# A transformer layer in split fp32: input rows kept on chip as the residual, and operand copies by ScalarE for the feed forward's block sums

## The chip, the cores and the metric

The kernel runs on one core of one Trainium2 chip. The core has five engines that run their own queues of instructions: TensorE (PE, matrix products; its weight loads are listed as PEld), VectorE (DVE), ScalarE (ACT), GpSimd (POOL) and SyncE (SP), which here only issues DMA. Engines wait for each other through semaphores; matrix products land in PSUM banks, everything else lives in SBUF. The metric is device microseconds of one launch.

## The reference

One layer on 512 tokens of width 1024, all in fp32:

```python
h = rms_norm(x, mix_norm_pre)
x = x + rms_norm(hybrid_mixer(h, ...), mix_norm_post)      # w_in, sparse attention, mLSTM, w_out
h = rms_norm(x, xattn_norm_pre)
x = x + rms_norm(memory_cross_attention(h, rms_norm(mem, mem_norm), ...), xattn_norm_post)
h = rms_norm(x, ffn_norm_pre)
g, u = jnp.split(h @ w_gate_up, 2, axis=-1)                # 1024 -> 2 x 2816
x = x + rms_norm((silu(g) * u) @ w_down, ffn_norm_post)
```

The mixer multiplies h by w_in, runs sparse attention over half of the columns and a chunked mLSTM over the other half, and multiplies by w_out. The cross attention reads 256 memory tokens.

## The kernel before

**Products in split fp32.** An fp32 operand is kept as a high and a low part of type fp32r: `split` has ScalarE copy the source to the high part (L166) and VectorE or GpSimd subtract that from the source for the low part (L167). A product is then three matmuls: low times high, high times low, high times high (L285 to L287 in `mm3`, L1210 to L1212 in `product`). Names that end in h or l are the parts: wah and wal (the small columns of w_in), wmh (its mLSTM value columns), hTh and hTl (the normalised input, transposed), wh and wl (a feed forward weight), A and AS (feed forward operands, both parts in one tile).

**Tiles and order.** The 512 tokens are four tiles of 128. The program is written in the order of the computation, and the Tile framework's scheduler, which simulates a time line, then sets the order in each engine's queue. Buffers come from pools with a fixed count; a tile that takes over a buffer waits until the former owner's last reader is done. A table, `PLAN`, holds strings that choose by position which engine does a step: v is VectorE, p is GpSimd.

**The head.** `load_x` has SyncE load the four row tiles of x into two tiles of a pool named S, which has six buffers (`slot`). `prenorm` normalises a row tile: ScalarE squares it and sums the row (L241), the reciprocal root is formed with GpSimd (L235), then for each half of 512 columns either VectorE scales it by root and gain in one pass (L249), or, where the plan says p, ScalarE scales it (L246) and GpSimd multiplies by the gain (L247). TensorE transposes the eight 128 x 128 squares into two PSUM banks (L253, tile name bk_pn), and `H.store` splits each bank into the transposed operand. In the head that operand is hT, four tiles from the same six S buffers, and mvx, the mLSTM values, is another S tile. The first products that use hT are bk_A (w_in's small columns, weights wah and wal) and bk_mv (weights wmh). The input rows are not kept: for the residual the ScalarE queue loads x a second time, into two tiles x1, by the DMA at L1026. That load has no wait, so the scheduler puts it at the start of the queue.

**The feed forward.** `ev_second2` ends the cross attention for a row tile (`post_second`, with the residual update at L282) and runs `prenorm` with the plan string norm3 into the operand A. A has four blocks, 11, 12, 21, 22: token half times feature half, each with both parts. The gate and up weights come in eleven column blocks. Block 0 multiplies A directly. Blocks 1 to 10 (`gate_up(d)`) use a scheme with seven products in place of eight for a 2 x 2 block product: besides 11, 12 and 22 they read four sums of the blocks, S1 = 21 + 22, S2 = S1 - 11, S3 = 11 - 21, S4 = 12 - S2, and sums of the weights (L1257 and its like, on VectorE). Each weight is split as it is needed, most on VectorE; the weights for block 12 (`w21`) and for S3 (`ulo`) are split by GpSimd. The raw weights sit in two pools of two buffers, `fraw[d % 2]`. SyncE loads block d + 2's into a pool when block d's are done with.

`A.sums(i)` forms the S operands for each row tile of 128 tokens. For that it first rebuilds the unsplit blocks by adding the two parts again: GpSimd does 11 and 12 (tile aq, L1186), VectorE does 21 and 22 (tile ar, L1183 and L1186). Row tiles 0 and 1 are the first token half, 2 and 3 the second, and the sums pair tile i with tile i + 2.

After the gate_up blocks come the products with w_down, and a last norm. They are not touched by the change.

Of the kernel before, what the change touches and what calls it, by code (L numbers as in the profile page):

```python
# [8 lines left out]
F32 = mybir.dt.float32  # L9
F32R = mybir.dt.float32r  # L10
AF = mybir.ActivationFunctionType
OP = mybir.AluOpType
AX = mybir.AxisListType

P = 128
S = 512
D = 1024
NT = S // P
# [28 lines left out]
def hybrid_layer(ctx, tc, a, out):  # L47
    nc = tc.nc
# [3 lines left out]
    xp = ENT(tc.tile_pool(name="xp", bufs=2))  # L52
# [22 lines left out]

# [3 lines left out]

# [38 lines left out]
    def norms_on_pool(name):  # L118

        return [(q // 2, q % 2) for q in range(8) if PLAN[name][q] == "p"]  # L120
# [4 lines left out]
    POOL1, POOL2, POOL3 = (norms_on_pool("norm%d" % n) for n in range(1, 4))  # L125
    x, mem = a["x"][0], a["mem"][0]
# [3 lines left out]
    def bank(tag, name=None):  # L130

        if tag == "b":
            tag = "pv" if turn[0] % 4 == 3 else "sc"
            turn[0] += 1
        return ps.tile([P, 512], F32, tag=tag, name=name or "bk_" + tag, bufs=BUFS[tag])

    def slot(shape, dt=F32, name="slot"):
        return sl.tile(shape, dt, tag="S", name=name)
# [22 lines left out]
    def small(shape, name, bufs=2):  # L161
        return sm.tile(shape, F32, tag=name, name=name, bufs=bufs)
# [75 lines left out]
    def prenorm(xi, i, gain, H, tag="tr", pool=(), take=None):  # L238
        ss = small([P, 1], "ss", 4)
        xn = (take or x4)([P, D], name="xn")  # L240
        nc.scalar.activation(xn, xi, AF.Square, scale=1.0 / 32.0, accum_out=ss)  # L241
        r = rstd_of(ss, 1)
        for g in range(2):
            c = slice(512 * g, 512 * g + 512)
            if (i, g) in pool:
                nc.scalar.activation(xn[:, c], xi[:, c], AF.Copy, scale=r)  # L246
                nc.gpsimd.tensor_tensor(xn[:, c], xn[:, c], gain[g], op=OP.mult)  # L247
            else:
                nc.vector.scalar_tensor_tensor(xn[:, c], xi[:, c], r, gain[g], op0=OP.mult, op1=OP.mult)  # L249
            b = bank(tag, "bk_pn")  # L250
            for k in range(4):
                kk = 4 * g + k
                nc.tensor.transpose(b[:, 128 * k:128 * k + 128], xn[:, 128 * kk:128 * kk + 128], ident)  # L253
            b3 = b.rearrange("p (k t) -> p k t", k=4)
            H.store(g, 128 * i, 128 * i + 128, b3)
# [108 lines left out]
    H = Big()  # L364
# [8 lines left out]
    mvx = slot([P, NT, 4, 129], name="mvx")  # L373
    nc.gpsimd.memset(mvx[:, :, :, 128:129], 1.0)
    wa, wm = [], []
    xin = [None] * NT

    def load_x(i):
        if i % 2 == 0:
            xin[i] = slot([P, 2, D], name="xin")  # L380
            xin[i + 1] = xin[i][:, 1, :]
            xin[i] = xin[i][:, 0, :]
        nc.sync.dma_start(xin[i], x[128 * i:128 * i + 128, :])

    def load_a(g):
        raw = rawt([P, 4, 288])
# [27 lines left out]
    g_in = []  # L414
# [36 lines left out]
        return nB[h][:, last:r0 + 1:step][:, ::-1]  # L451

    for i in range(NT):
        prenorm(xin[i], i, g_in, H, pool=POOL1)
    nc.sync.dma_start(gb, a["mlstm_gate_bias"][0].rearrange("(o i) h -> o (i h)", o=1).to_broadcast([P, 8]))
    nc.sync.dma_start(rows[0:16], a["conv_w"][0].rearrange("w (c p) -> (w c) p", p=P))
    nc.sync.dma_start(rows[16:20], a["conv_b"][0].rearrange("(c p) -> c p", p=P))
# [82 lines left out]
    for j in range(NT):  # L540
        for i in range(j, NT):
            idx[i, j] = len(idx)
            c = 4 * idx[i, j]
            src = ir[:, 128 * j:128 * j + 128]
            if i > j:
# [6 lines left out]
                src = t  # L552
# [416 lines left out]
    def comp_loads(n):  # L969
        for g in range(2):  # L970
            comp_load(n, g)

    whole = {"c0": lambda: conv(0), "c1": lambda: conv(1),
             "m0": lambda: start("m0", 2336, 2, H, ev_mo(0)), "m2": lambda: start("m2", 2336 + 256, 2, H, ev_mo(2)),
             "kc": lambda: start("kc", 512, 2, H, ev_kcvc),
             "ks": lambda: start("ks", (768, 1024), 2, H, lambda j, b: ev_k(j)(0, b)),
             "q0": lambda: start("q0", 0, 2, H, ev_q(0)),
             "Ck": lambda: comp("k"), "Cv": lambda: comp("v")}
    begun = {}
    for op in PLAN["order"].split():  # L980
# [4 lines left out]
        else:  # L985
            n = op[1]
# [34 lines left out]

    g_post = gain_bc(a["mix_norm_post"])
    g_pre = gain_bc(a["xattn_norm_pre"])
    x1 = [xp.tile([P, 2, D], F32, tag="x1", name="x1") for _ in range(2)]
    for i in range(2):
        nc.scalar.dma_start(x1[i], x[256 * i:256 * i + 256, :].rearrange("(i p) c -> p i c", p=P))  # L1026

    def res(i):
        return x1[i // 2][:, i % 2, :]

    w_out = a["w_out"][0]
    first = {}

# [80 lines left out]
    fraw = [pool("fr0", 2, "right")]  # L1114
# [8 lines left out]
    def weights(src, eng=None):  # L1123
        w = wtile(name="wh"), wtile(name="wl")
        split(*w, src, eng)
        return w
# [10 lines left out]
    def gtile(shape=(P, 2, 512), name="gf"):  # L1137
        return fg.tile(list(shape), F32, tag="gf", name=name)
# [4 lines left out]
    class Blocks:  # L1143
# [29 lines left out]
        def store(self, g, c0, c1, src):  # L1173
            i = c0 // 128
            self.put("%d%d" % (i // 2 + 1, g + 1), i, src)

        def whole(self, o, n, i, eng):

            c = slice(128 * (i % 2), 128 * (i % 2) + 128)
            if n == "21":  # L1180
                for k in (0, 2):
                    h, l = (self.piece(n, q, k)[:, :, c].bitcast(F32) for q in range(2))
                    eng.tensor_tensor(o[:, k:k + 2], h, l, op=OP.add)  # L1183
            else:
                h, l = (self.c[n][:, q, :, c].bitcast(F32) for q in range(2))
                eng.tensor_tensor(o, h, l, op=OP.add)  # L1186

        def sums(self, i):
            q, r, s = (gtile((P, 2, 4, 128), name=n) for n in ("aq", "ar", "as"))
            for n in range(2):  # L1190
                self.whole(q[:, n], "1%d" % (n + 1), i, nc.gpsimd)
                self.whole(r[:, n], "2%d" % (n + 1), i, nc.vector)
            nc.vector.tensor_tensor(s[:, 0], r[:, 0], r[:, 1], op=OP.add)
            nc.vector.tensor_tensor(s[:, 1], s[:, 0], q[:, 0], op=OP.subtract)
            self.put("S2", i, s[:, 1])
            self.put("S1", i, s[:, 0])
            nc.vector.tensor_tensor(r[:, 0], q[:, 0], r[:, 0], op=OP.subtract)
            self.put("S3", i, r[:, 0])
            nc.vector.tensor_tensor(q[:, 1], q[:, 1], s[:, 1], op=OP.subtract)
            self.put("S4", i, q[:, 1])  # L1200

    def product(b, w, n, start, stop=True):

# [22 lines left out]
    A = Blocks()  # L1226
# [2 lines left out]

    w_first = [weights(q) for q in load_gu(0)]  # L1230

    def ev_second2(i, b):
        post_second(first[i], b, g_post2, res(i), res(i), pn=sgran)
        prenorm(res(i), i, g_pre2, A, pool=POOL3, take=ntile)
# [11 lines left out]
    def gate_up(d):  # L1246

        glo, ghi, ulo, uhi = load_gu(d)
        X, Y = bank("sc", "bk_X"), bank("d", "bk_Y")
        product(X, weights(glo), "11", True)  # L1250
        x1 = etile(name="x1")
        nc.scalar.activation(x1, X, AF.Copy)
        w21 = weights(ghi, nc.gpsimd)
        t1 = ft.tile([P, 4, 256], F32, tag="t1", name="t1")
        nc.vector.tensor_tensor(t1, ulo, glo, op=OP.subtract)
        nc.vector.tensor_tensor(ulo, uhi, ulo, op=OP.subtract)
        nc.vector.tensor_tensor(glo, ulo, glo, op=OP.add)  # L1257
        product(Y, w21, "12", True)
        nc.vector.tensor_tensor(x1, x1, Y, op=OP.add)
        nc.scalar.activation(x1, x1, AF.Silu)  # L1260
        product(X, weights(glo), "S2", False)
        u2 = etile(name="u2")
        nc.scalar.activation(u2, X, AF.Copy)  # L1263
        Z = bank("pv" if d % 2 else "tr", "bk_Z")
        product(Z, weights(t1), "S1", True)
        p5 = etile(name="p5")
        nc.scalar.activation(p5, Z, AF.Copy)
        nc.vector.tensor_tensor(ghi, ghi, glo, op=OP.subtract)  # L1268
        product(X, weights(ulo, nc.gpsimd), "S3", False)
        nc.vector.tensor_tensor(p5, p5, X, op=OP.add)  # L1270
        product(Z, weights(uhi), "S4", False)
        nc.vector.tensor_tensor(u2, u2, Z, op=OP.add)
        Gf[d] = gtile()
        nc.gpsimd.tensor_tensor(Gf[d][:, :, 0:256], halves(x1), halves(u2), op=OP.mult)
        product(X, weights(ghi), "22", False)
        s2 = etile(name="s2")
        nc.scalar.activation(s2, X, AF.Silu)
        nc.gpsimd.tensor_tensor(Gf[d][:, :, 256:512], halves(s2), halves(p5), op=OP.mult)

    Gf[0] = gtile()  # L1280
    for t in range(2):
# [4 lines left out]
        s1 = etile(name="s1")  # L1286
        nc.scalar.activation(s1, gate, AF.Silu)
        nc.vector.tensor_tensor(Gf[0][:, :, 256 * t:256 * t + 256], halves(s1), halves(up), op=OP.mult)
    for i in range(2, NT):
        A.sums(i)  # L1290
    for d in range(1, NF // 2):
        gate_up(d)

# [6 lines left out]
    for g in range(NF // 2):  # L1300
        raw = fraw[1 - g // 2 % 2].tile([P, 2, D], F32, tag="raw", name="raw")
        nc.sync.dma_start(raw, wd[:, 2 * g:2 * g + 2, :])
        for q in range(2):
            k = 2 * g + q
# [11 lines left out]
            for i in range(NT):  # L1316
                t = slice(128 * i, 128 * i + 128)
                for n in range(2):
                    c = slice(512 * n, 512 * n + 512)
                    mm3(bk[i][n], gs[:, 0, t], gs[:, 1, t], hi[:, c], lo[:, c], k == 0, False)  # L1320
    for i in range(NT):
        t = slice(128 * i, 128 * i + 128)
        for n in range(2):
            c = slice(512 * n, 512 * n + 512)
# [4 lines left out]
        for n in range(2):  # L1329
            c = slice(512 * n, 512 * n + 512)  # L1330
# [30 lines left out]
```

## Time and profile before

| | us |
|---|---|
| three runs | 860.01, 865.17, 865.51 |
| median | 865.17 |
| the profiled execution | 864.1 |
| its span | 862.3 |

The profiled execution had 12,664 instructions and a mean granted clock of TensorE of 0.99. The page cuts the span into 40 slices of 21.6 us; a digit is the busy share of an engine in a slice, in tenths (9 is 90% or more), and PEclk is the clock that TensorE was granted. These lines give the shape of the whole program: the head is the first slice or two, the feed forward starts in the 24th and ends with the last.

```profile
PE   5899999998999999999999988999999999999997
DVE  3528687688879835843453689788888884323413
ACT  5423565667857743733453435444554444324311
POOL 3405133255437542511320255444444445322420
PEclk9999998999999999999999999999999999999999
DMA  8633332331102242252341330333333333322101
```

TensorE is under 0.9 in the first two slices, in one in the mixer (the 10th), around the opening of the feed forward, and at the very end. In the timeline view a row has the start, the time in us, the engine (a name with q is that engine's issue of DMA or its sequencer), the line, the operation, out<-in, the size, and in brackets the idle time ahead of it with what ended it. Rows of like instructions in a row are joined (x2), and their time is then that of all.

### The profile page before, as it was taken

How to read it: one execution, taken by the hardware profiler on the slowest of the kernel's cores; microseconds unless marked ns; L12 is line 12 of the kernel's file. 1: busy time of each engine (PE TensorE's matmuls, PEld its weight loads, DVE VectorE, ACT ScalarE, POOL GpSimd, SP SyncE). 2: the span in 40 equal slices, each digit the busy share in tenths (PEclk: the TensorE clock that was granted, in tenths of full speed). 3: DMA queues.
4: the chain of work that ended last, by engine and by line, in shares of the span. 5: the costliest groups of instructions: out<-in, count | busy, mean ns of one | idle time of the engine just before them, and what ended most of it. 6: DMA issues, size and time to landing. Idle time of an engine off the chain costs nothing. (4 is left out here: it accounts for less than half of the span.)

```text
span 862.3 us, 12664 instructions
## 1 busy us (share of the span) xinstructions
PE 822.5 (95%) x4833; PEld 707.7 (82%) x4833; DVE 543.1 (63%) x925; ACT 424.3 (49%) x838; POOL 326.9 (38%) x238
## 2 busy tenths in 40 slices
PE   5899999998999999999999988999999999999997
PEld 3787677885688978778888887999999999888885
DVE  3528687688879835843453689788888884323413
ACT  5423565667857743733453435444554444324311
POOL 3405133255437542511320255444444445322420
PEclk9999998999999999999999999999999999999999
DMA  8633332331102242252341330333333333322101
GB/s 274 208 110 115 84 91 62 105 103 50 52 24 84 98 139 72 80 165 69 127 147 49 102 119 1 99 98 98 99 107 116 115 122 130 99 98 98 50 25 73
DMA packets 68307, 85.27 MB, mean 99 GB/s; under 512 B 4400, under 2 KB 53905, under 8 KB 68246
## 3 DMA queue, kind: packets, MB, share of 16 engines
q1 hardware_dynamic: 64574, 77.97, 27.9%
q10 hardware_dynamic: 3672, 6.50, 2.2%
q8 instruction: 38, 0.62, 0.3%
q14 instruction: 23, 0.19, 0.1%
HBM read 82.34 MB, written 2.12 MB: 98 GB/s over the span
## 5 line engine op out<-in xcount | busy, mean ns | idle before, releaser
L166 ACT ACTIVATE whi<-raw 128x1024 fp32r<-128x1024 f32 (+1 forms) x80 | 76.8, 967 | 69.6 <-PE bk_dT L285 31.9
L167 DVE TENSOR_TENSOR wlo<-raw,whi 128x1024 fp32r<-128x1024 f32 x41 | 55.0, 1343 | 80.1 <-PE bk_ff L286 43.0
L166 ACT ACTIVATE wh<-raw 128x1024 fp32r<-128x1024 f32 x64 | 67.3, 1057 | 60.6 <-PE bk_X L1210 24.5
L167 POOL TENSOR_TENSOR wl<-raw,wh 128x1024 fp32r<-128x1024 f32 x20 | 62.8, 3143 | 89.9 <-ACT wh L166 89.9
L167 POOL TENSOR_TENSOR wlo<-raw,whi 128x1024 fp32r<-128x1024 f32 x23 | 56.2, 2443 | 93.9 <-ACT whi L166 92.1
L285 PE MATMUL bk_dT<-hTh,wlo 128*128 128x512 f32 x192 | 77.4, 403 | 1.4 <-DVE wlo L167 0.8
L287 PE MATMUL bk_dT<-hTh,whi 128*128 128x512 f32 x192 | 76.8, 400 | 0.0
L286 PE MATMUL bk_dT<-hTl,whi 128*128 128x512 f32 x192 | 76.6, 399 | 0.0
L167 DVE TENSOR_TENSOR wl<-raw,wh 128x1024 fp32r<-128x1024 f32 x44 | 63.3, 1444 | 10.3 <-ACT wh L166 10.3
L167 POOL TENSOR_TENSOR gs<-gf,gs 128x512 fp32r<-128x512 f32 x22 | 32.8, 1498 | 65.4 <-ACT gs L166 65.4
L1210 PE MATMUL bk_X<-A,wl 128*128 128x256 f32 x192 | 54.4, 283 | 0.5 <-ACT A L166 0.5
L1211 PE MATMUL bk_X<-A,wh 128*128 128x256 f32 x192 | 54.4, 283 | 0.3 <-DVE A L167 0.3
L1212 PE MATMUL bk_X<-A,wh 128*128 128x256 f32 x192 | 54.2, 283 | 0.0
L1210 PE MATMUL bk_X<-AS,wl 128*128 128x256 f32 x160 | 46.2, 289 | 4.4 <-ACT u L1263 2.4
L286 PE MATMUL bk_ff<-wlo,gs 128*128 128x512 f32 x128 | 49.8, 389 | 0.0
L287 PE MATMUL bk_ff<-whi,gs 128*128 128x512 f32 x128 | 49.6, 389 | 0.0
L285 PE MATMUL bk_ff<-whi,gs 128*128 128x512 f32 x128 | 47.4, 389 | 0.0
L891 POOL TENSOR_SCALAR s<-s,acf 128x128 f32<-128x128 f32 (+3 forms) x32 | 36.3, 1145 | 25.6 <-PE bk_tr L906 15.9
L1212 PE MATMUL bk_X<-AS,wh 128*128 128x256 f32 x160 | 45.6, 285 | 0.0
L1211 PE MATMUL bk_X<-AS,wh 128*128 128x256 f32 x160 | 45.5, 285 | 0.0
L285 PEld LDWEIGHTS bk_dT<-hTh,wlo 128*128 128x128 f32 x192 | 36.3, 189 | 10.8 <-DVE wlo L167 1.9
L1210 PE MATMUL bk_Z<-AS,wl 128*128 128x256 f32 x160 | 45.0, 281 | 0.0
(375 smaller groups left out, 2566.8 us busy)
## 6 DMA issues: line engine op xcount, KB each, us to landing
raw<-in_w_gate_up_dram SPq DMA_DIRECT2D x22, 1024.0 KB, 5.6
raw<-in_w_down_dram SPq DMA_DIRECT2D x11, 1024.0 KB, 5.3
raw<-in_w_xkv_dram SPq DMA_DIRECT2D x8, 1024.0 KB, 5.0
raw<-in_w_in_dram SPq DMA_DIRECT2D x7, 1024.0 KB, 6.1
raw<-in_w_out_dram SPq DMA_DIRECT2D x4, 1024.0 KB, 5.2
raw<-in_w_xq_dram SPq DMA_DIRECT2D x4, 1024.0 KB
raw<-in_w_xo_dram SPq DMA_DIRECT2D x4, 1024.0 KB, 5.1
raw<-in_w_in_dram SPq DMA_DIRECT2D x6, 512.0 KB, 4.0
```

What stands on the lines that cost most here:

```text
L166: nc.scalar.activation(hi, src, AF.Copy)
L167: (eng or nc.vector).tensor_tensor(lo, src, hi.bitcast(F32), op=OP.subtract)
L285: nc.tensor.matmul(o, lhsT=wl, rhs=xh, start=start, stop=False)
L286: nc.tensor.matmul(o, lhsT=wh, rhs=xl, start=False, stop=False)
L287: nc.tensor.matmul(o, lhsT=wh, rhs=xh, start=False, stop=stop)
L891: ENG[on].tensor_scalar(s[:, 0:n], s[:, 0:n], c, None, op0=OP.mult)
L1210: nc.tensor.matmul(o, lhsT=wl[:, k, c], rhs=A.hi(n, k), start=st, stop=False, skip_group_check=True)
L1211: nc.tensor.matmul(o, lhsT=wh[:, k, c], rhs=A.lo(n, k), start=False, stop=False, skip_group_check=True)
L1212: nc.tensor.matmul(o, lhsT=wh[:, k, c], rhs=A.hi(n, k), start=False, stop=stop and k == 3, skip_group_check=True)
```

## The change

Two parts.

First, the rows of x are loaded into two tiles `xres` of the pool that held x1, and `res(i)` reads them from the start of the program: `prenorm` of the head normalises them, and the later residual update adds to them in place. The second load and the tiles x1 are gone, and the two input tiles of the S pool with them.

Second, in the opening of the feed forward, norm3 becomes "vvvvvvvv": all eight half tiles of that norm are scaled by VectorE in one pass, none by ScalarE and GpSimd. `Blocks.store`, besides the split, has ScalarE copy the PSUM bank as it is into a tile `aw`. The two aw tiles are taken from the raw weight pool of the even blocks, `fraw[0]`. `Blocks.whole()` with its additions is gone, and `sums()`, now called once for all tiles, forms the four sums on VectorE from aw, S3 and S4 in place. For block 1 alone the split of `w21` moves from GpSimd to VectorE.

```diff
-        "norm3": "vpvpppvv",
+        "norm3": "vvvvvvvv",
...
-    xin = [None] * NT
+    xres = [xp.tile([P, 2, D], F32, tag="x", name="xin") for _ in range(2)]
+
+    def res(i):
+
+        return xres[i // 2][:, i % 2, :]

     def load_x(i):
-        if i % 2 == 0:
-            xin[i] = slot([P, 2, D], name="xin")
-            xin[i + 1] = xin[i][:, 1, :]
-            xin[i] = xin[i][:, 0, :]
-        nc.sync.dma_start(xin[i], x[128 * i:128 * i + 128, :])
+        nc.sync.dma_start(res(i), x[128 * i:128 * i + 128, :])
...
-        prenorm(xin[i], i, g_in, H, pool=POOL1)
+        prenorm(res(i), i, g_in, H, pool=POOL1)
...
-    x1 = [xp.tile([P, 2, D], F32, tag="x1", name="x1") for _ in range(2)]
-    for i in range(2):
-        nc.scalar.dma_start(x1[i], x[256 * i:256 * i + 256, :].rearrange("(i p) c -> p i c", p=P))
...
         def store(self, g, c0, c1, src):
             i = c0 // 128
             self.put("%d%d" % (i // 2 + 1, g + 1), i, src)
+            nc.scalar.activation(self.whole[i // 2][:, i % 2, g], src, AF.Copy)

-        def whole(self, o, n, i, eng):
...
-        def sums(self, i):
-            q, r, s = (gtile((P, 2, 4, 128), name=n) for n in ("aq", "ar", "as"))
-            for n in range(2):
-                self.whole(q[:, n], "1%d" % (n + 1), i, nc.gpsimd)
-                self.whole(r[:, n], "2%d" % (n + 1), i, nc.vector)
...
+        def sums(self):
+            q, r = self.whole
+            s = [gtile((P, 2, 4, 128), name="as") for _ in range(2)]
+            for i in range(2):
+                nc.vector.tensor_tensor(s[i][:, 0], r[:, i, 0], r[:, i, 1], op=OP.add)
+                nc.vector.tensor_tensor(s[i][:, 1], s[i][:, 0], q[:, i, 0], op=OP.subtract)
+                self.put("S2", i, s[i][:, 1])
+            for i in range(2):
+                self.put("S1", i, s[i][:, 0])
+            for i in range(2):
+                nc.vector.tensor_tensor(r[:, i, 0], q[:, i, 0], r[:, i, 0], op=OP.subtract)
+                self.put("S3", i, r[:, i, 0])
+            for i in range(2):
+                nc.vector.tensor_tensor(q[:, i, 1], q[:, i, 1], s[i][:, 1], op=OP.subtract)
+                self.put("S4", i, q[:, i, 1])
...
+    A.whole = [fraw[0].tile([P, 2, 2, 4, 128], F32, tag="raw", name="aw") for _ in range(2)]
...
-        w21 = weights(ghi, nc.gpsimd)
+        w21 = weights(ghi, nc.vector if d == 1 else nc.gpsimd)
...
-    for i in range(2, NT):
-        A.sums(i)
+    A.sums()
```

The scheduler lays the queues out anew. Between the head and the feed forward's opening the order stays as it was. In the listings below, lines of the changed kernel are numbered in its own file, up to 15 less than before.

ScalarE's queue at the head; rows with - stand only before, with + only after. gain is a gain row spread over the partitions, xin an input row tile, bk_pn a bank of transposed squares.

```order
-L1026 DMA x_3425<-in_x_dram 128x2x1024
-L1026 DMA x_3426<-in_x_dram 128x2x1024
 L419 ACTIVATE gain<-bk_g 128x512
 L241 ACTIVATE xn,ss<-xin 128x1024
 L419 ACTIVATE gain<-bk_g 128x512
 L246 ACTIVATE xn<-xin,rs_r 128x512
-L166 ACTIVATE hTh<-bk_pn 128x4x128 x2
-L166 ACTIVATE wah<-raw 128x288 x8
+L166 ACTIVATE wah<-raw 128x288 x4
+L166 ACTIVATE hTh<-bk_pn 128x4x128
+L166 ACTIVATE wah<-raw 128x288 x4
+L166 ACTIVATE hTh<-bk_pn 128x4x128
```

The two DMAs are gone, and the splits of wah moved ahead of those of the first two banks of hT, four before each.

ScalarE's queue as the feed forward opens, before, around the splits of row tiles 0 and 1. A_ with a number is a block of A, pn,ss the square of the cross attention's output for its norm, x_ with a number the residual rows.

```order
L166 ACTIVATE A_4812<-bk_pn 128x4x128
L258 ACTIVATE pn,ss_4986<-bk_dR 128x512
L246 ACTIVATE xn<-x_3425,rs_r 128x512
L166 ACTIVATE A_4813<-bk_pn 128x4x128
L241 ACTIVATE xn,ss<-x_3426 128x1024
L258 ACTIVATE pn,ss_5049<-bk_dR 128x512
L166 ACTIVATE A_4812<-bk_pn 128x4x128
L246 ACTIVATE xn<-x_3426,rs_r 128x512 x2
L166 ACTIVATE A_4813<-bk_pn 128x4x128
L241 ACTIVATE xn,ss<-x_3426 128x1024
```

And the same stretch after:

```order
L166 ACTIVATE A_4808<-bk_pn 128x4x128
L166 ACTIVATE A_4809<-bk_pn 128x4x128
L258 ACTIVATE pn,ss_4986<-bk_dR 128x512
L1169 ACTIVATE aw<-bk_pn 128x512 x2
L241 ACTIVATE xn,ss<-xin 128x1024
L258 ACTIVATE pn,ss_5049<-bk_dR 128x512
L166 ACTIVATE A_4808<-bk_pn 128x4x128
L166 ACTIVATE A_4809<-bk_pn 128x4x128
L1169 ACTIVATE aw<-bk_pn 128x512 x2
L241 ACTIVATE xn,ss<-xin 128x1024
```

The scaling passes of L246 are gone; the two copies to aw (L1169) stand behind the high parts of both banks, ahead of the next row tile's row sum.

VectorE's queue at the start of block 1, before. ar, aq and as are the rebuilt blocks and their sums, AS_ with a number an S operand, raw the weights and their sums, gf the output of a feed forward block.

```order
L167 TENSOR_TENSOR AS_5099<-ar,AS_5099 128x4x128
L1257 TENSOR_TENSOR raw<-raw 128x1024
L167 TENSOR_TENSOR AS_5098<-as,AS_5098 128x4x128
L1199 TENSOR_TENSOR aq<-aq,as 128x512
L167 TENSOR_TENSOR AS_5100<-aq,AS_5100 128x4x128
L167 TENSOR_TENSOR AS_5097<-as,AS_5097 128x4x128
L1288 TENSOR_TENSOR gf<-s_5301,bk_Y 128x2x256
L167 TENSOR_TENSOR AS_5099<-ar,AS_5099 128x4x128
L1268 TENSOR_TENSOR raw<-raw 128x1024
L167 TENSOR_TENSOR wl<-raw,wh 128x1024
```

And after:

```order
L167 TENSOR_TENSOR wl<-raw,wh 128x1024
L167 TENSOR_TENSOR AS_5101<-aw,AS_5101 128x4x128
L167 TENSOR_TENSOR AS_5099<-as,AS_5099 128x4x128
L167 TENSOR_TENSOR AS_5101<-aw,AS_5101 128x4x128
L167 TENSOR_TENSOR AS_5102<-aw,AS_5102 128x4x128
L167 TENSOR_TENSOR wl<-raw,wh 128x1024
L1244 TENSOR_TENSOR raw<-raw 128x1024
L167 TENSOR_TENSOR AS_5102<-aw,AS_5102 128x4x128
L1275 TENSOR_TENSOR gf<-s_5303,bk_Y 128x2x256
L1255 TENSOR_TENSOR raw<-raw 128x1024
L167 TENSOR_TENSOR wl<-raw,wh 128x1024
```

The sums' low parts now come from aw, and of the splits of weights (wl) among them one more belongs to VectorE, w21 of block 1.

More of the change, by code (lines that the diff above doesn't have):

```diff
@@ L1023, in hybrid_layer @@
     g_pre = gain_bc(a["xattn_norm_pre"])
-    x1 = [xp.tile([P, 2, D], F32, tag="x1", name="x1") for _ in range(2)]
-    for i in range(2):
-        nc.scalar.dma_start(x1[i], x[256 * i:256 * i + 256, :].rearrange("(i p) c -> p i c", p=P))
-    def res(i):
-        return x1[i // 2][:, i % 2, :]
     w_out = a["w_out"][0]
@@ L1175, in store @@
             self.put("%d%d" % (i // 2 + 1, g + 1), i, src)
-        def whole(self, o, n, i, eng):
[L1179 to L1186, printed above, removed]
-        def sums(self, i):
-            q, r, s = (gtile((P, 2, 4, 128), name=n) for n in ("aq", "ar", "as"))
-            for n in range(2):
-                self.whole(q[:, n], "1%d" % (n + 1), i, nc.gpsimd)
-                self.whole(r[:, n], "2%d" % (n + 1), i, nc.vector)
[L1193 to L1200, printed above, removed]
+            nc.scalar.activation(self.whole[i // 2][:, i % 2, g], src, AF.Copy)
[14 more added lines that the diff above has]
+                self.put("S4", i, q[:, i, 1])
     def product(b, w, n, start, stop=True):
```

## The prediction

> **What bounds the kernel now.** I read the profile's page first: busy shares, then the chain that ended last. TensorE works nearly all the time and carries the chain; every other engine has room.
>
> ```profile
> PE 822.5 (95%) x4833; PEld 707.7 (82%) x4833; DVE 543.1 (63%) x925; ACT 424.3 (49%) x838; POOL 326.9 (38%) x238
> PE 37%; DVE 3%; issue 1%; ACT 1%; DVEq 0%; POOLq 0%; POOL 0%; ACTq 0%
> ```
>
> So an edit is worth what it takes from TensorE's idle time (862.3 - 822.5 = 39.8 us) or from stretches where its clock is cut. The view by windows, cut where TensorE's timeline changes, shows these (columns: stretch, length, then busy us and count for PE, PEld, DVE, ACT, POOL, then granted clock, DMA share, GB/s).
>
> ```profile
> 0.00:13.00 13.00, 5.95 (x12) 2.59 (x12) 2.05 (x7) 5.96 (x10) 2.58 (x8) 1.00 0.91 294
> 13.00:19.20 6.20, 3.81 (x13) 3.05 (x14) 2.81 (x8) 5.40 (x14) 3.94 (x6) 1.00 0.90 300
> 42.40:500.00 457.60, 443.97 (x2319) 359.38 (x2318) 297.45 (x692) 252.79 (x592) 164.37 (x142) 0.99 0.29 95
> 509.00:513.20 4.20, 4.19 (x23) 4.20 (x24) 3.10 (x5) 1.92 (x4) 0.66 (x1) 0.60 0.01 2
> 536.00:540.40 4.40, 4.40 (x25) 4.40 (x26) 4.40 (x5) 0.89 (x2) 0.00 (x0) 0.63 0.00 0
> 540.40:560.60 20.20, 20.20 (x171) 20.20 (x171) 15.64 (x12) 9.00 (x11) 9.80 (x4) 1.00 0.33 105
> ```
>
> Two places are not bound by TensorE: the head, which waits for loads (DMA at 0.9), and the opening of the feed forward, 507 to 540, where VectorE is full. Between them TensorE is 97% busy, so a head that ends earlier moves everything behind it. From 540 on there is nothing to win. The change touches just these two places.
>
> **Part 1, the residual stays on chip.** Two 1 MB loads leave ScalarE's queue and two input tiles leave the six "S" slots. No instruction replaces them. The timeline of the head, by engine:
>
> ```profile
> 1.70 1.01 ACTq L1026 DMA_DIRECT2D x<-in_x_dram  x2
> 4.67 3.04 SPq L388 DMA_DIRECT2D raw<-in_w_in_dram  x1
> 19.44 0.94 SPq L398 DMA_DIRECT2D raw<-in_w_in_dram  x2
> 12.67 1.44 ACT L166 ACTIVATE wah<-raw 128x288 fp32r<-128x288 f32 x4 [1.77 <-DMA raw<-in_w_in_dram]
> 24.69 1.15 ACT L166 ACTIVATE wmh<-raw 128x512 fp32r<-128x512 f32 x2 [3.82 <-DMA raw<-in_w_in_dram]
> 7.02 0.72 ACT L246 ACTIVATE xn<-xin,rs_r 128x512 f32<-128x512 f32 x1 [0.18 <-POOL rs_r L235]
> 10.30 0.60 ACT L166 ACTIVATE hTh<-bk_pn 128x512 fp32r<-128x512 f32 x1 [0.70 <-PE bk_pn L253]
> 9.63 0.69 DVE L167 TENSOR_TENSOR hTl<-bk_pn,hTh 128x512 fp32r<-128x512 f32 x1 [1.86 <-ACT hTh L166]
> 19.14 0.69 DVE L167 TENSOR_TENSOR hTl<-bk_pn,hTh 128x512 fp32r<-128x512 f32 x1
> 13.16 0.61 PE L285 MATMUL bk_A<-wah,hTl 128*128 128x288 f32 x1 [2.90 <-ACT wah L166]
> 14.06 0.44 PE L287 MATMUL bk_A<-wah,hTh 128*128 128x288 f32 x1
> 14.30 0.44 PE L285 MATMUL bk_A<-wah,hTl 128*128 128x288 f32 x1
> 19.15 1.09 PE L253 MATMUL bk_pn<-cc,xn 128*128 128x128 f32 x4 [2.23 <-ACT xn L246]
> 22.93 1.91 PE L253 MATMUL bk_pn<-cc,xn 128*128 128x128 f32 x8
> ```
>
> The two loads for x go out at 1.7, ahead of the small-row pieces of wah's weights, and SP's own issue at 4.67 is held up for 3 us. At the 300 GB/s of the windows 2.1 MB is 7 us of transfers; the head moves 5.7 MB by 19.2 (294 GB/s for 13.0 us, 300 for 6.2). ScalarE could split wah as soon as its earlier work ends, near 7.8 (7.02 + 0.72) instead of 12.67. The second row of hTl is the slot: the fourth tile of hT is written at 19.14 although its high part was ready at 10.9, because it takes over the slot of the input rows. Without that, tile 0's 24 matmuls run in one piece from near 10.4 (hTl's first half) for 24 x 0.24 = 5.8 us (the pitch of the rows at 14.06 and 14.30), to 16.2; now they end at 22.93. That is 6.7 us, the upper end. TensorE then waits for wmh: the order puts one matmul on wmh ahead of tile 1, so it blocks there until that load has landed. Its two issues at 19.44 wait for the wal splits and for the input rows; both should come some 6 us earlier, with 5.3 us to land as now, so wmh is there near 18. Lower end: if the small rows set the pace themselves, only the 2.23 us wait at 19.15 goes. I take 5.0, nearer the upper end, because the loads and the slot point the same way.
>
> **Part 2, the opening of the feed forward.** TensorE's stalls there, and what the work behind them took:
>
> ```profile
> 509.01 0.63 PE L253 MATMUL bk_pn<-cc,xn 128*128 128x128 f32 x4 [2.02 <-DVE A L167]
> 514.31 0.29 PE L1210 MATMUL bk_X<-A,wl 128*128 128x256 f32 x1
> 525.84 0.28 PE L1210 MATMUL bk_X<-A,wl 128*128 128x256 f32 x1
> 530.83 0.39 PE L1210 MATMUL bk_Y<-A,wl 128*128 128x256 f32 x1 [1.96 <-POOL wl L167]
> 535.99 0.36 PE L1210 MATMUL bk_X<-AS,wl 128*128 128x256 f32 x1 [2.01 <-DVE wl L167]
> 483.08 0.75 DVE L249 SCALAR_TENSOR_TENSOR xn<-x,rs_r,gain 128x512 f32<-128x512 f32 x1 [0.66 <-POOL rs_r L235]
> 497.33 3.47 DVE L282 SCALAR_TENSOR_TENSOR x<-yo,rs_r,x 128x512 f32<-128x512 f32 x2
> 502.83 3.48 DVE L249 SCALAR_TENSOR_TENSOR xn<-x,rs_r,gain 128x512 f32<-128x512 f32 x2 [0.66 <-POOL rs_r L235]
> 531.26 3.45 DVE L1268 TENSOR_TENSOR raw<-raw 128x1024 f32<-128x1024 f32 x1
> 502.76 6.90 POOL L1186 TENSOR_TENSOR aq<-A 128x512 f32<-128x512 f32 x4
> L167 POOL TENSOR_TENSOR wl<-raw,wh x8: 2391/3128/8887, 521.9 to 597.6; 128x1024 fp32r<-128x1024 f32 x8
> L1183 DVE TENSOR_TENSOR ar<-A,A x4: 417/420/420, 515.1 to 517.5; 128x256 f32<-128x256 f32 x4
> L1186 DVE TENSOR_TENSOR ar<-A x2: 683/684/686, 515.8 to 517.8; 128x512 f32<-128x512 f32 x2
> L166 ACT ACTIVATE A<-bk_pn 128x512 fp32r<-128x512 f32 x6 | 3.6, 592 | 0.7 <-PE bk_pn L253 0.7
> L246 ACT ACTIVATE xn<-x,rs_r 128x512 f32<-128x512 f32 x4 | 2.8, 719 | 0.8 <-POOL rs_r L235 0.8
> L167 DVE TENSOR_TENSOR wl<-raw,wh 128x1024 fp32r<-128x1024 f32 x8 | 9.6, 1218 | 1.5 <-ACT wh L166 1.5
> ```
>
> A VectorE pass of 0.75 us (483.08) takes 1.74 when GpSimd works beside it (497.33, 502.83: 3.48 for two), and the 1.22 us pass takes 3.45 at 531.26. GpSimd pays too: its slowest split took 8.89 us against a median of 3.13; the first starts at 521.9, and 521.9 + 8.9 is 530.8, where TensorE's wait for it ends.
>
> VectorE loses four 0.42 and two 0.68 us adds (3.0) and gains four norm halves (3.0) and one split (1.2): 1.2 us more. GpSimd loses 6.9 us of adds, four norm passes and that split. With them go VectorE's delays: 2 x 1.0 at 497, 2 x 1.0 at 502.8 and 2.2 at 531, or 6.2. ScalarE loses four 0.72 us passes and gains eight copies of 0.59: 4.7 - 2.9 = 1.8 more, on an engine that is idle over half of the stage. In its queue a copy waits for VectorE's low part of the same bank, and the next tile's row sum stands behind it; it also frees that bank later.
>
> Laid out by these durations in the new order: tile 2's two norm halves and yo stand ahead of tile 1's low split on VectorE, so TensorE starts the feed forward 0.7 us later than now. Tile 3's transposes then need a bank that ScalarE's copies free near 507.3 and TensorE asks near 508.9: no stall, 2.02 saved. The next products start near 511.3 instead of 514.31, their 96 matmuls take the same 11.5 us, and block 1 starts near 522.8 instead of 525.84. VectorE, by then with eleven sums and splits (0.6 apart) and one weight split behind it, has wl at 519.7; w21, now on VectorE, at 523.3, asked at 525.7: 1.96 saved. The S2 weights come at 528.4, asked at 528.6: 2.01 saved, but with only 0.2 to spare. Without the idle time the cut clock should go: 4.2 x 0.40 + 4.4 x 0.37 = 3.3. The S3 weights remain on GpSimd: from near 529, 3.1 us if VectorE leaves gaps, 8.9 if not; asked near 534.4, so a stall of 0 to 3.5. I take 1.0, nearer the median of eight than its maximum.
>
> On the clock, the Trainium skill (TensorE: Matmul & The Clock Gate, Part 1) says the array drops to half rate after an idle window of about 3.4 us. Here 2.0 us of waiting stands ahead of a stretch at 0.60, so the trace disagrees and decides; by the page these waits would not be the cause, the 3.3 would stay, and the time would be some 3 us higher.
>
> Sum: 5.0 + (2.02 + 1.96 + 2.01) + 3.3 - 0.7 - 1.0 = 12.6 us. The profiled execution took 864.1, so 851.5; the median of the three runs shown, 865.17, lies 1.1 above it, so 852.5 on the scale of the median.
>
> **The rivals.**
> Only the second part pays (head worth 2.2): 864.1 - 9.8 + 1.1 = 855.5. For it: the head's loads have small rows. Against: the late hTl at 19.14.
>
> GpSimd's S3 split starves behind a VectorE that is never free, the full 3.5 us, and its idle time cuts the clock for another 1.6: 5.1 in place of 1.0, 856.6. For it: the 8.89 us split, in the same place and against the same full VectorE. Against: VectorE waits for ScalarE's high parts there, which opens gaps. The Trainium skill (SBUF — State Buffer, Who interferes with whom) has a VectorE instruction with two SBUF inputs and a reading GpSimd instruction exclude each other for a whole instruction, whichever issues first. The trace agrees: 1.74 against 0.75 above. By that rule moving one split to VectorE does not free the one that stays.
>
> Slower: the two tiles that hold ScalarE's copies take the buffers into which block 2's weights were prefetched at 476.6; their load can start only once the S4 splits are done, near 525, and lands 5 to 6 us later.
>
> ```profile
> 476.59 2.64 SPq L1221 DMA_DIRECT2D raw<-in_w_gate_up_dram  x2
> raw<-in_w_gate_up_dram SPq DMA_DIRECT2D x22, 1024.0 KB, 5.6
> ```
>
> Block 2 asks for them near 537, so 6 us are to spare; each us beyond is one of TensorE's. The gain of 12.6 is used up when they land at 550, which needs sums 19 us late; slower by over 1% needs 27. With sums 30 us late, as when ScalarE's copies and VectorE's low parts hold each other's banks, the loss is 24 us and the time 876.
>
> No gain anywhere (the loads and VectorE were not what held TensorE): 865. Against it, the rows of waits above.
>
> **How the numbers follow.** The forecast has 0.56, the weak head 0.17, the starved split 0.14, both of these together (859.6) 0.05, no gain 0.03, slower 0.05. Range: the best case is 6.7 + 6.0 + 3.3 - 0.7 = 15.3 (849.9), and single runs here lie within 0.3% (2.6 us), so 847; at the other end 859.6 with 1 us of that, so 860.5. About 1% (8.6 us) is what a measurement of this kernel can tell from no change. Faster by more than that needs 856.5: the forecast, the weak head and a bit of the third, 0.74; slower 0.05; the rest 0.21.
>
> **What would show it.** Right: wah split before 10, no gap ahead of the second bk_pn, the head's work some 5 us earlier at 45; no TensorE stall over 1 us between 500 and 540, clock 1.00 there, VectorE's L249 and L282 at 0.75, no aq. Wrong: wah still waiting for DMA near 12; TensorE waiting for aw's bank, for POOL wl at S3, or for block 2's raw; or a middle stretch that takes back what the head won.

## The result and the profile after

| | before | after |
|---|---|---|
| median us | 864.05 (4 runs, 860.01 to 865.51) | 849.86 (4 runs, 848.59 to 849.94) |
| span of the profiled execution | 862.3 | 848.1 |
| ratio of times | | 0.984, 95% interval 0.9803 to 0.9876 |

The changed kernel is 14.2 us faster. 852.5 had been forecast, with a range from 847.0 to 860.5. One execution of `norm3_only` (below) took 1604.35 us and is left out of its ratio. The busy shares of the changed kernel's page (engine, busy us, share of the span, instructions):

```profile
PE 816.0 (96%) x4833; PEld 703.6 (83%) x4833; DVE 536.6 (63%) x924; ACT 426.1 (50%) x842; POOL 307.1 (36%) x229
```

TensorE still bounds the kernel. Its idle time is 848.1 - 816.0 = 32.1 us against 39.8, and its busy time fell by 6.5 us although it runs the same 4,833 matmuls: fewer of them ran at a slow clock. To place the gain I read the start of the same instruction in both traces. The first row of the table stands behind all products of the head in both orders; the third is behind all products of feed forward block 0.

| start of | before | after | gained so far |
|---|---|---|---|
| a small product of the mixer (bk_rb) | 62.5 | 58.4 | 4.1 |
| the feed forward's first product | 496.63 | 491.07 | 5.6 |
| block 1 | 525.84 | 517.18 | 8.7 |
| block 1's product with S2 | 535.99 | 523.18 | 12.8 |
| block 2's product with 12 | 554.73 | 540.30 | 14.4 |
| end of the span | 862.3 | 848.1 | 14.2 |

The head and the opening of the feed forward make the gain, as forecast. The 1.5 us between the first two rows fall in the middle, whose order did not change. From bk_rb to the feed forward's first product it took 434.1 us before and 432.7 after, and 432.2 to 434.8 in eleven other profiles below in which TensorE's order there is the same but for four instructions at its end; so this 1.5 need not be the change's.

**The head.** In the changed kernel, ScalarE's first split of the small-column weights, TensorE's rows with a wait, and what VectorE and GpSimd did ahead of the long one, from the timelines by engine:

```profile
8.20 1.45 ACT L166 ACTIVATE wah<-raw 128x288 fp32r<-128x288 f32 x4 [0.65 <-DMA raw<-in_w_in_dram]
10.90 0.61 PE L285 MATMUL bk_A<-wah,hTl 128*128 128x288 f32 x1 [0.84 <-DVE hTl L167]
16.71 1.03 PE L253 MATMUL bk_pn<-cc,xn 128*128 128x128 f32 x8
18.51 0.50 PE L285 MATMUL bk_mv<-wmh,hTl 128*128 128x512 f32 x1 [0.77 <-ACT wmh L166]
22.78 1.12 PE L253 MATMUL bk_pn<-cc,xn 128*128 128x128 f32 x4 [3.77 <-DVE hTl L167]
18.70 3.42 DVE L249 SCALAR_TENSOR_TENSOR xn<-xin,rs_r,gain 128x512 f32<-128x512 f32 x2 [0.46 <-POOL rs_r L235]
22.05 0.68 DVE L167 TENSOR_TENSOR hTl<-bk_pn,hTh 128x512 fp32r<-128x512 f32 x1
18.64 2.94 POOL L167 TENSOR_TENSOR wml<-raw,wmh 128x512 fp32r<-128x512 f32 x2
```

The split starts at 8.20 in place of 12.67. Row tile 0's 24 matmuls run in one piece from 10.90 and end ahead of the transposes at 16.71; before, they ran from 13.16 to 22.93 with a hole in them. But then there is a new wait of 3.77 us: the low part of row tile 1 (hTl, 22.05) stands on VectorE behind row tile 3's norm (18.70), and that norm's two passes took 3.42 us, beside two splits of GpSimd that began 0.06 us earlier. The windows show what followed (columns as in the prediction, the clock is the third number from the end):

```profile
16.70:19.00 2.30, 1.53 (x11) 0.99 (x9) 1.84 (x5) 2.10 (x7) 0.95 (x3) 1.00 1.07 383
19.00:22.80 3.80, 0.03 (x2) 0.02 (x1) 3.80 (x5) 1.58 (x4) 2.58 (x2) 0.63 0.36 116
22.80:24.20 1.40, 1.40 (x7) 1.40 (x8) 1.40 (x3) 0.27 (x1) 0.00 (x0) 0.50 0.00 0
24.20:27.00 2.80, 2.80 (x13) 2.76 (x13) 2.54 (x4) 2.41 (x5) 1.35 (x1) 0.54 0.39 96
```

TensorE is empty for 3.8 us and then works at half clock until near 27. The new wait costs what the old ones did: from its first bk_A product to bk_rb TensorE stands idle for 4.5 us in both kernels (4.47 before, 4.54 after).

**The opening of the feed forward.** TensorE's rows at the places of the five waits before (first product, its second matmul, row tile 3's transposes, product with 12, product with S2), GpSimd's split for S3, and the product that uses it:

```profile
491.07 0.39 PE L1195 MATMUL bk_X<-A,wl 128*128 128x256 f32 x1 [0.39 <-ACT A L166]
492.55 0.39 PE L1196 MATMUL bk_X<-A,wh 128*128 128x256 f32 x1 [0.97 <-DVE A L167]
503.12 0.60 PE L253 MATMUL bk_pn<-cc,xn 128*128 128x128 f32 x4
520.06 0.28 PE L1195 MATMUL bk_Y<-A,wl 128*128 128x256 f32 x1
523.18 0.38 PE L1195 MATMUL bk_X<-AS,wl 128*128 128x256 f32 x1
523.84 3.39 POOL L167 TENSOR_TENSOR wl<-raw,wh 128x1024 fp32r<-128x1024 f32 x1 [27.37 <-DVE x L1246]
528.91 0.28 PE L1195 MATMUL bk_X<-AS,wl 128*128 128x256 f32 x1
503.00:517.00 14.00, 14.00 (x120) 14.00 (x119) 12.36 (x21) 9.01 (x16) 0.00 (x0) 1.00 0.00 1
517.00:540.00 23.00, 22.92 (x193) 22.72 (x193) 21.48 (x19) 11.60 (x14) 8.13 (x3) 1.00 0.56 183
```

The three waits of 2 us are gone (ahead of a row without a bracket the engine was idle for under 0.15 us), TensorE is busy from 503 to 540 but for 0.08 us, and the clock stays at 1.00. GpSimd's split for S3 ends at 523.84 + 3.39 = 527.2, 1.7 us before TensorE asks for it.

### The profile page after: what moved, and what is told of

The parts are those of the page before. It is cut to its first block, busy times and chain, and to the rows that moved or that the text cites. A ratio compares the mean times of both kernels' runs of the same rounds, so it can differ in the third digit from the quotient of the medians.

```text
span 848.1 us, 12643 instructions
## 1 busy us (share of the span) xinstructions
PE 816.0 (96%) x4833; PEld 703.6 (83%) x4833; DVE 536.6 (63%) x924; ACT 426.1 (50%) x842; POOL 307.1 (36%) x229
## 4 chain that ended last, share of the span: by engine, by line
PE 79%; DVE 11%; ACT 5%; issue 2%; DMA 1%; POOL 1%; SPq 1%; DVEq 0%; ACTq 0%; POOLq 0%
PE bk_X L1195 5%; PE bk_X L1196 5%; PE bk_X L1197 5%; PE bk_ff L285 5%; PE bk_ff L287 5%; PE bk_ff L286 5%; PE bk_dT L285 4%; PE bk_dT L286 4%; PE bk_dT L287 4%; PE bk_pv L921 3%; PE bk_dN L286 3%; PE bk_dN L285 3%; PE bk_dN L287 3%; PE bk_Z L1195 2%; PE bk_Z L1196 2%; PE bk_Z L1197 2%
## 5 line engine op out<-in xcount | busy, mean ns | idle before, releaser
L167 POOL TENSOR_TENSOR wl<-raw,wh 128x1024 fp32r<-128x1024 f32 x19 | 55.5, 2923 | 97.2 <-ACT wh L166 69.8
L167 DVE TENSOR_TENSOR wl<-raw,wh 128x1024 fp32r<-128x1024 f32 x45 | 65.6, 1463 | 9.2 <-ACT wh L166 9.2
L891 POOL TENSOR_SCALAR s<-s,acf 128x128 f32<-128x128 f32 (+3 forms) x32 | 36.3, 1145 | 25.6 <-PE bk_tr L906 15.9
```

The costliest lines, as they stand in the source:

```text
L167: (eng or nc.vector).tensor_tensor(lo, src, hi.bitcast(F32), op=OP.subtract)
L891: ENG[on].tensor_scalar(s[:, 0:n], s[:, 0:n], c, None, op0=OP.mult)
```

## The experiments

Where two kernels are compared within the feed forward, I use the stretch from its first product to the end of the span, since the head and the middle differ by 1 to 3 us from run to run. It took 365.7 us before, 357.0 after, and 356.9 when the changed kernel was run again.

### The two parts apart

`resid_only` is the kernel before with the first part of the diff, `ff_only` with the second.

> The first part alone (input rows kept as the residual, the feed forward as before). If the two parts add up, the head's 5.4 us (495.06 before, 489.64 after, at the same transposes) come alone: about 858.6 us, and the feed forward's waits of 2.02, 1.96 and 2.01 us stand as before. Rival: the head's gain needs the second part, or is taken back before the end: 864.

> The second part alone (x loaded twice as before). If the parts add up, 14.2 - 5.4 = 8.8 us come: about 855.3 us, no wait of TensorE over 1 us as the feed forward opens, granted clock 1.00 there. Rival: the new order of the opening only fits when the head is early too: one of the three waits is left, 857 or more.

`resid_only` took 857.91 us against 864.55 for the kernel before on the same chip (ratio 0.9926, 0.9904 to 0.9949), `ff_only` 855.25 (0.9892, 0.987 to 0.9914). Both expectations held: 6.6 and 9.3 us, which add up to 15.9 against the 14.2 of the whole. The waits of TensorE in the two stretches, first of `resid_only` as the feed forward opens (columns: who waited for what, us in total, times, longest):

```profile
PE bk_pn L253 <- DVE A L167: 2.0, 1, 2.0
PE bk_X L1203 <- DVE wl L167: 2.0, 1, 2.0
PE bk_Y L1203 <- POOL wl L167: 2.0, 1, 2.0
```

and of `ff_only` there:

```profile
PE bk_X L1203 <- DVE A L167: 1.0, 1, 1.0
PE bk_X L1202 <- ACT u L1257: 0.4, 1, 0.4
PE bk_X L1202 <- ACT A L166: 0.4, 1, 0.4
```

The stretch takes 364.3 us in `resid_only` and 357.0 in `ff_only`. The second part's gain is in the feed forward and needs nothing of the first. `resid_only` has the same three waits as the kernel before and is still 1.4 us shorter there: only one of its waits was followed by a cut clock, against two before (the last section says why). That is most of the 1.7 us by which the two parts exceed the whole.

### The head: the transfers or the slot

```diff
 # load_later, on the kernel before
     for i in range(2):
+        nc.vector.tensor_copy(x1[i][:, 0, 0:1], Ym[0][:, 0, 0:1].bitcast(F32))
         nc.scalar.dma_start(x1[i], x[256 * i:256 * i + 256, :].rearrange("(i p) c -> p i c", p=P))
 # load_again, on the changed kernel
+    dm = slot([P, 2, D], name="dm")
+    nc.scalar.dma_start(dm, x[0:256, :].rearrange("(i p) c -> p i c", p=P))
+    for i in range(4):
+        dg = gran((P, 512), name="dg")
+        nc.scalar.dma_start(dg, x[256 + 128 * (i // 2):384 + 128 * (i // 2), 512 * (i % 2):512 * (i % 2) + 512])
     load_x(0)
```

> The kernel before, with the second load of x held back until the mixer's end; the six S slots still hold the input rows. If the transfers alone made the head late, the small-column weights are split near 8 us in place of 12.67, and the whole 5.4 us come: 858.6. If the slot did it, the second half of the first low part still waits for it near 19 and at most 2 us come: 862 or more.

> The changed kernel, with 2 MB of x loaded once more by ScalarE's queue at the start, into tiles that nothing reads; no S slot is held by input rows. If the transfers alone made the head late, all 5.4 us are given back: 855.3. If the slot did it, less than 2 us are given back: below 852.

`load_later` took 859.32 us against 864.55 (0.993, 0.9901 to 0.9959); its feed forward begins at 491.96, 4.7 us earlier than before. That understates its head: bk_rb starts at 53.50, 9.0 us earlier, and 4.4 are lost behind it. There TensorE's order differs from before in 115 of 2,188 places, and a wait of 4.64 us up to 194.4 goes with a stretch of 10.24 us at half clock. The slot was still held, but the second half of the first low part came at 14.98 and not near 19 as I expected: with the input rows landing earlier, the slot came free earlier. `load_again` took 851.63, 0.8 to 1.8 us more than the changed kernel's two medians (849.86, 850.79); its feed forward begins at 492.41. In each run the theory held whose cause had been removed, so neither alone is right: with the transfers gone and the slot still held the head gains, and with the slot free and the transfers still there it gains most of the same. In `load_again` the 24 matmuls start late, at 13.79, but run in one piece and the transposes behind them follow at 19.89:

```profile
13.79 0.61 PE L285 MATMUL bk_A<-wah,hTl 128*128 128x288 f32 x1 [1.02 <-ACT wah L166]
19.89 0.63 PE L253 MATMUL bk_pn<-cc,xn 128*128 128x128 f32 x4 [0.31 <-DVE xn L249]
```

The two runs speak for both mechanisms of the prediction. How the gain divides between them is not shown, since the scheduler laid out the queues of the head anew in both runs. They do not add, because in the changed kernel something else ends last in the head. The next experiment is on that.

### The head: what ends last now

`after_wm_vector` is the changed kernel with one entry of the plan changed; `after_again` is the changed kernel, run beside the second copy of it.

```diff
-        "wm": "ppvvvpvv",
+        "wm": "vvvvvvvv",
```

> The changed kernel with the head's value weights (wml) all split by VectorE, none by GpSimd. TensorE's new wait of 3.77 us at 22.78 is for a low part that stands on VectorE behind row tile 3's norm, whose two passes took 3.42 us beside GpSimd's two splits. If that is contention, they take 1.4 to 1.5 us, the wait falls by 2 us and some of the clock cut behind it (0.50 to 0.63 from 19 to 27) goes: 846 to 848. Rival: the order on VectorE sets the wait, or the splits that VectorE takes on come late: 850 or more.

> The changed kernel once more, on the chip of the next run, for comparison with it: 849 to 851.

> The changed kernel with all value weights (wml) split by VectorE, beside the changed kernel on one chip. If the 2.0 us that the norm of row tile 3 gains on VectorE reach the end, it is 1.5 to 3 us below the run before this one; rival: the earlier run was a lucky one, and the two lie within 1 us.

Side by side on one chip, `after_wm_vector_again` took 847.01 us (ratio to the kernel before 0.98, 0.9785 to 0.9814) and `after_again` 850.79 (0.9843, 0.9827 to 0.9859). The intervals do not overlap: 3.8 us are to be had on top of the change, somewhat more than expected. The first run gave 848.20 (0.9815, 0.9793 to 0.9836). VectorE's rows in `after_wm_vector`:

```profile
18.67 1.41 DVE L249 SCALAR_TENSOR_TENSOR xn<-xin,rs_r,gain 128x512 f32<-128x512 f32 x2 [0.47 <-POOL rs_r L235]
20.00 0.68 DVE L167 TENSOR_TENSOR hTl<-bk_pn,hTh 128x512 fp32r<-128x512 f32 x1
```

Row tile 3's norm takes 1.41 us in the same place where it took 3.42, and the low part behind it starts at 20.00 in place of 22.05. The order on VectorE up to that row is the same, so it was contention. Behind it the scheduler laid out the queues anew, so the 3.8 us are those of the whole edit. The cut clock has a part in them: behind the long wait it lasts 6.83 us in `after` and `after_again`; the two runs of `after_wm_vector` show none and 3.41 us. The other kernels with the early head form a series, since GpSimd's two splits wait for a weight load that lands at slightly different times (`load_later` stands last, its order is another):

| kernel | GpSimd's splits begin | norm of row tile 3: begins, took | bk_rb begins | feed forward begins |
|---|---|---|---|---|
| after_sums_old | 18.52 | 18.55, 3.46 | 58.08 | 492.86 |
| after | 18.64 | 18.70, 3.42 | 58.42 | 491.07 |
| after_again | 18.64 | 18.70, 3.42 | 59.34 | 492.86 |
| resid_only | 18.94 | 18.94, 3.49 | 59.21 | 491.54 |
| after_w21_gpsimd | 19.13 | 18.60, 2.44 | 58.27 | 491.93 |
| after_norm3_old | 19.81 | 18.78, 1.42 | 56.23 | 489.26 |
| after_wm_vector | none | 18.67, 1.41 | 54.55 | 488.47 |
| after_wm_vector_again | none | 18.61, 1.41 | 56.05 | 488.25 |
| load_later | 18.77 | 18.72, 3.59 | 53.50 | 491.96 |

If GpSimd starts first, both passes of the norm are held up; if VectorE is half a microsecond ahead, the pass under way is not and only the next one is; if GpSimd comes a microsecond late, neither. Below some 0.05 us the starts do not tell who had the turn: in `resid_only` the two begin together, in `load_later` VectorE is 0.05 us ahead, and both passes are held up. In `load_later` TensorE waits for that low part only 0.33 us, as other work stands ahead in its queue. A weight load that landed later (ScalarE's split of wmh at 19.10 in `after_norm3_old`, at 17.84 in the changed kernel) went with a faster head; the half of the contention that is left in `after_w21_gpsimd` still went with a late bk_rb. The Trainium skill (SBUF — State Buffer, Who interferes with whom) says that a VectorE instruction with two SBUF inputs and a GpSimd instruction that reads SBUF take turns, the one that issues first keeping the port for its whole length. The first eight rows of the table fit that rule; for `load_later` the starts on record do not show which instruction issued first.

### The feed forward: which of three edits

The second part has three edits. Each was made alone on the kernel before or undone alone in the changed kernel: the plan of the third norm (`norm3_only`, `after_norm3_old`), block 1's w21 (`after_w21_gpsimd`), and the copies with the sums (`sums_only`, `after_sums_old`).

```diff
 # norm3_only, on the kernel before (after_norm3_old: the reverse, on the changed one)
-        "norm3": "vpvpppvv",
+        "norm3": "vvvvvvvv",
 # after_w21_gpsimd, on the changed kernel
-        w21 = weights(ghi, nc.vector if d == 1 else nc.gpsimd)
+        w21 = weights(ghi, nc.gpsimd)
 # sums_only, on the kernel before (after_sums_old: the reverse, on the changed one)
+            nc.scalar.activation(self.whole[i // 2][:, i % 2, g], src, AF.Copy)
...
-        def whole(self, o, n, i, eng):
...
-    for i in range(2, NT):
-        A.sums(i)
+    A.sums()
```

> The kernel before with the third norm wholly on VectorE, nothing else. If the feed forward's opening gains by several causes, each with its own wait, GpSimd's additions (6.9 us beside the norm of row tile 3) and its weight split stay and so do the waits of 1.96 and 2.01 us; the 2.02 us wait goes at most: 860 to 864. Rival: the norm's passes on GpSimd were what slowed VectorE, and all 8.8 us come: 855.

> The changed kernel with the third norm's plan as before (four half tiles on ScalarE and GpSimd). If the norm's passes matter, VectorE's passes beside them take 1.7 us in place of 0.75 again and a wait of TensorE returns: 852 to 854. Rival: the copies and the split carry it all, and the time stays within 1 us of 849.9.

> The changed kernel with block 1's w21 split by GpSimd again. If GpSimd's split starves beside a full VectorE whatever else is gone, it takes near 9 us from about 513, is done near 522 where TensorE asks at 520.1, and the wait of about 2 us is back: 852, or 853.5 with the clock cut. Rival: it begins early enough or VectorE leaves it gaps: 849.9.

> The kernel before with ScalarE's copies and the new sums alone: third norm, w21 and the second load of x as before. Measured from the feed forward's first product to the end of the span (365.7 us before, 357.0 after), undoing the norm in the changed kernel cost nothing and undoing w21 cost about 0.6. If the copies and sums carry the opening, this stretch takes 357 to 358.5 us and the kernel 855 to 857. Rival: three small parts that need each other: 361 and 860 or more.

> The changed kernel with the operand rebuilt from its parts again (GpSimd 6.9 us, VectorE 3.0 us), no copies by ScalarE; the norm and w21 stay on VectorE. If copies and sums carry the opening, waits of TensorE of 2 us or more are back there: 361 to 363 us from the first product to the end, 853 to 856 in all. Rival: norm and w21 on VectorE do it without them: below 852.

| kernel | median us | ratio to before, interval | first product to end | gained of 8.6 | TensorE's waits from tile 3's transposes to S2 | stretches at half clock |
|---|---|---|---|---|---|---|
| before | | | 365.7 | | 2.02, 1.96, 2.01 | 2 |
| norm3_only | 861.30 | 0.9962, 0.9937 to 0.9986 | 361.8 | 3.9 | 0.3, 0.8, 2.2 | 1 |
| sums_only | 857.57 | 0.9926, 0.9901 to 0.9951 | 359.0 | 6.7 | 1.1, 1.6 | 0 |
| after_sums_old | 852.69 | 0.9868, 0.9854 to 0.9882 | 359.2 | 6.5 | 0.3, and 1.3 at S1 | 0 |
| after_w21_gpsimd | 851.04 | 0.9846, 0.9828 to 0.9865 | 357.6 | 8.1 | 0.7 | 0 |
| after_norm3_old | 850.12 | 0.9828, 0.9806 to 0.985 | 356.7 | 9.0 | none | 0 |
| after | 849.86 | 0.984, 0.9803 to 0.9876 | 357.0 | 8.6 | none | 0 |

The stretches are those of one profiled execution each. For `norm3_only` (857.36 us) and `after_norm3_old` (847.71) it was the shortest of all, so their 3.9 and 9.0 may be too large. The copies and the sums alone bring 6.7 of the 8.6 us; the norm and w21 without them (`after_sums_old`) bring 6.5. Undone in the changed kernel the norm costs nothing (my expectation of 852 to 854 was wrong, the rival held) and w21 0.6 us (I expected 2), too little to show in the whole times. `norm3_only` alone came out where I expected it, but the wait for GpSimd's split shrank with it, from 1.96 to 0.8. For `sums_only` and `after_sums_old` the outcome lies between my theory and its rival. What they share is the clock: the two half-clock stretches, 3.3 us, went with either set. Waits of 1.1 and 1.6 us in `sums_only` drew none.

GpSimd's split of w21 in `after_w21_gpsimd` shows that the starvation is real while its price is small:

```profile
515.11 6.59 POOL L167 TENSOR_TENSOR wl<-raw,wh 128x1024 fp32r<-128x1024 f32 x1 [17.77 <-ACT wh L166]
521.75 0.39 PE L1195 MATMUL bk_Y<-A,wl 128*128 128x256 f32 x1 [0.68 <-POOL wl L167]
```

It takes 6.59 us beside a full VectorE, against a median of 3.13 before. But it starts 6.0 us ahead of TensorE's request (521.75 - 0.68 = 521.07), where in the kernel before it started 7.0 ahead and took 8.9.

## Why the prediction was right, and where it was off

- **Head, 5.0 us taken, 2.2 to 6.7 as ends.** The measured gain at bk_rb is 4.1 us. The steps held: the wah split at 8.20 (7.8 forecast), the 24 matmuls in one piece from 10.90 to 16.7 (10.4 to 16.2), wmh split at 17.84 (18). What the sum missed is the 3.77 us wait that took the place of the old ones. The earlier weight load brought GpSimd's splits beside row tile 3's norm; in the kernel before that norm ran alone. The prediction named this contention in the feed forward and did not look for it in the head. Without it (`after_wm_vector`) the feed forward begins 2.6 to 4.6 us earlier than in the two profiles of the changed kernel, near or beyond the upper end. At the end of row tile 0's matmuls the changed kernel is 6.2 us ahead (16.71 against 22.93), close to the upper end too; by bk_rb, behind the wait and the cut clock, 4.1 of that are left.
- **The three stalls, 5.99 us.** All gone. The layout put block 1 at 522.8 on the old head, and 522.8 - 5.6 = 517.2 is where it is. It gave each stall its own cause, though, and the experiments show overlap: either the copies and sums or the norm and w21 take most of it away, and the norm's passes are worth nothing once the rest is there.
- **The cut clock, 3.3 us.** Right in these two profiles: both cuts went with the waits. That there were two to win was luck in part. In `resid_only` the same three waits (2.03, 1.97, 1.99) drew one cut, as the last section explains, and the prediction had no term for where a wait falls.
- **The later start, 0.7 us.** The two first waits grew from 0.54 + 0.34 to 0.39 + 0.97, so 0.5.
- **The S3 split, 1.0 us.** The mis-sized term: no wait. GpSimd got its turn after one pass of VectorE and took 3.39 us, near the median that the prediction leaned to; the delay fell on VectorE's next weight split (3.43 us where 1.2 is usual), for which nobody waited.
- **Sum.** Forecast 12.6; spans say 14.2, of which 1.5 fell in the unchanged middle. The mechanism was right; that the errors of the head and of S3 nearly cancel is luck. (The price of the weak head adds up to 855.4, not 855.5.)
- **Rivals.** The weak head and the starved S3 split did not occur. Block 2's weights were issued at 516.3, some 9 us before the 525 that the slower case assumed, and no wait for them shows.

## What to carry to other kernels

When a change lets a load land earlier, look at what the work behind that load will now run beside, above all GpSimd beside VectorE passes that the critical queue stands behind; one entry of a plan won 3.8 us here on top of a change that had already gained 14. Where several edits remove waits of the same stretch, do not add their prices: make each alone and undo each alone, since either set may take away the same clock cut. Where the part ahead of a stage varies from run to run, measure that stage from a fixed instruction of its own.

## What the runs showed of the hardware

- **Whether a wait of 2.0 us cuts the clock depends on where it falls.** In each of the fourteen traces the cuts at 0.50 begin whole multiples of 3.413 us apart, from the head to the end (before: 509.83 and 537.13 are eight apart), and each lasts 3.41 us or a multiple, unless the program ends in it. A cut of 3.41 us costs 1.7. Laid on this grid, the nine waits of the opening fall into two kinds:

| kernel | waits that lie whole in one stretch of the grid | cut begins | waits that a boundary divides | cut |
|---|---|---|---|---|
| before | 2.02, 2.01 | 509.83, 537.13 | 1.44 + 0.52 | none |
| resid_only | 1.99 | 529.85 | 0.66 + 1.37, 0.78 + 1.20 | none |
| load_later | 2.03, 1.99 | 504.72, 532.02 | 0.98 + 0.99 | none |

  So it is TensorE's idle time within one stretch that counts. Over all fourteen traces, from the first clock record on, of the stretches that were not cut themselves, 37 had more than 1.75 us of it and a cut followed every one; 3,294 had less than 1.35 and none followed; of the 31 between, 15 were followed. The Trainium skill (TensorE: Matmul & The Clock Gate, Part 1) describes a free-running window of about 3.4 us; the length of a cut and the grid agree with that. Its idle time of at least a whole window does not: 2.0 us were enough.
- **The clock column does not show the slow start.** In the head, bk_A's matmuls of 288 columns follow each other every 0.24 us at a granted clock of 1.00, until 16.3 in the changed kernel, and every 0.13 us from 32 on. In the cut at 0.50, from 23.9 to 26.3, it is 0.24 again, so the first stretch looks like half speed as well. The trace's clock records begin only at 16.54 (25.13 before); the 1.00 ahead of them is no reading. These rows of its TensorE timeline show both paces:

```profile
11.30 0.44 PE L286 MATMUL bk_A<-wal,hTh 128*128 128x288 f32 x1
11.54 0.44 PE L287 MATMUL bk_A<-wah,hTh 128*128 128x288 f32 x1
...
32.22 0.29 PE L287 MATMUL bk_A<-wah,hTh 128*128 128x288 f32 x1
32.35 0.30 PE L285 MATMUL bk_A<-wah,hTl 128*128 128x288 f32 x1
```

  In the kernel before, the slow pitch lasts until 24.8. How much of the head's gain is that earlier warm-up was not tried apart.
- **Who starts first decides, as far as the profile resolves it.** A lead of 0.06 us of GpSimd's split over VectorE's pass cost VectorE 2.0 us; a lead of VectorE by 0.5 us cut that to 1.0; one of 0.05 us, in `load_later`, did not help it.
